# Gate and up of a feed-forward layer: seven block products for eight over half of the contraction

## Chip, cores and metric

One Trainium2 chip, one of its cores. The metric is the time of one execution on the device in microseconds (us). Engines: TensorE (PE; PEld is its weight load), VectorE (DVE), ScalarE (ACT), GpSimd (POOL) and SyncE (SP), which issues the loads of the weights.

## What is computed

One layer of a hybrid encoder for 256 tokens of width 2048, all in float32: a joint input projection, three mixers (a gated recurrence, a stick-breaking attention, a latent attention), an output projection with a residual, and the feed-forward layer that the change is about, whose inner width is 5632:

```python
x = x + jnp.concatenate([hg_out, sb_out, mla_out], axis=-1) @ w_o[layer]
h = rmsnorm(x, ffn_norm_g[layer])
x = x + (jax.nn.silu(h @ w_gate[layer]) * (h @ w_up[layer])) @ w_down[layer]
return rmsnorm(x, final_norm_g)
```

## The kernel before

**Products.** A float32 product is made of three products of a shorter format (float32r). Every operand is split into a rounded part `hi` and a rest `lo`, and `gemm_mm` (L143) sums hi x hi, hi x lo and lo x hi in PSUM (L151 to L153). The weights come in slabs of 256 rows by 512 columns, in SBUF a tile `raw` of 128 partitions x 2 x 512. `split_w` (L105) loads a slab on SyncE's queue (L116), ScalarE casts it to `hi` (L119) and VectorE subtracts to get `lo` (L91, the helper `tt`). There are four buffers each of `raw`, `hi` and `lo`. One slab is 12 products of 128x512: two blocks of 128 rows of tokens (`b`), two halves of the 256 rows (`j`), three products.

**Gate and up.** The inner width is walked in 11 groups of 512 columns. For each group `ff` runs eight slabs of w_gate into two accumulators, then eight slabs of w_up into two others (psA, four banks). ScalarE applies SILU to the gate sums (L835), with the row's norm factor `r2` as scale, VectorE multiplies with the up sums to `hh` (L94), and `turn_hid` transposes `hh` in eight 128x128 blocks (L246) and splits the result into `hi` and `lo` right away: a cast (L827) and a subtraction. A group is 16 slabs, so 192 products, and eight transposes.

**Around it.** The output projection ends in `wo_end`, which adds the residual into the tiles `x2` (R0 to R3), takes sums of squares and makes the transposed copy `x2T`, a tile of hi and lo for each 256 rows. Down (four column blocks of 22 slabs) reads the split hidden tiles and adds into x2; the final norm follows.

**What sets the order.** The program is written as one stream. The framework's scheduler puts each instruction on its engine's list and adds the waits; a buffer of a pool is taken in turn, and its next user waits until the last one is done. `split_w` works under a raised priority (L107, `ahead`), so that loads and splits stand earlier in the lists than the text has them. Small pieces of work (transposes) are kept as tasks that `tick` advances after every slab. An engine runs its list strictly in order. GpSimd has nothing to do in gate and up.

Of the kernel before, what the change touches and what calls it, by code (L numbers as in the profile page):

```python
# [52 lines left out]
SABBUFS = 3  # L53
WARM = 9
MAGIC = 12582912.0
LOGEXP = "natural_log_exp_and_others"


def build(tc, x, xT, pos, gains, fgain, lbraw, w_in, w_uq, w_ukv, w_o, w_gate, w_up, w_down, cst, msk, out, dbg=None):
# [41 lines left out]

# [75 lines left out]

# [1 line left out]
    gcol = cons.tile([P, G_END], F32, name="gcol")  # L179
# [10 lines left out]

# [1 line left out]
    zeros = big("sab", (P, 512), BF16, bufs=SABBUFS)  # L192
# [617 lines left out]

    # ==== gated feed-forward ====
    hid = {}

    def ff(w, c0):
        a = acc_tile()
        for i in range(8):
            gemm_slab(a, w, i * 256, c0, 512, x2T[i], i == 0, i == 7)
        return a

    def turn_hid(g, hh):  # L820
        yield
        for i in range(2):
            ps = transpose4([[hh[:, b, (2 * i + j) * P:(2 * i + j + 1) * P] for b in range(2)] for j in range(2)])
            n = 2 * g + i
            at = act_tile() if n < 8 else late.tile([P, 2, 2, 256], F32R, name=nm("ht"), tag="ht", bufs=14)
            pv = ps.rearrange("p (j n) -> p j n", j=2)
            act.copy(at[:, 0, :, :], pv)  # L827
            tt(at[:, 1, :, :], pv, at[:, 0, :, :].bitcast(F32), ALU.subtract)
            hid[n] = at

    for g in range(11):
        a = ff(w_gate, g * 512)
        sg = late.tile([P, 2, 512], F32, name=nm("sg"), tag="sg", bufs=1)
        for b in range(2):
            act.activation(sg[:, b, :], a[b], AF.Silu, scale=r2[:, b:b + 1])  # L835
        a = ff(w_up, g * 512)
        hh = late.tile([P, 2, 512], F32, name=nm("hh"), tag="hh", bufs=1)
        for b in range(2):
            stt(hh[:, b, :], a[b], r2[:, b:b + 1], sg[:, b, :], ALU.mult, ALU.mult)
        spawn(turn_hid(g, hh))  # L840

    gf = late.tile([P, D], F32, name="gf", bufs=1)
    sp.dma_start(gf, fgain.partition_broadcast(P))
    ss3 = sm(10, "ss3", 1)

    def settle(g, b, a, cs, col):
        tb = x2[g][:, b, cs]
        tt(tb, tb, a[b][:, cs], ALU.add)
        junk = late.tile([P, 512], F32, name=nm("junk"), tag="junk", bufs=1)
        act.activation(junk[:, cs], tb, AF.Square, accum_out=ss3[:, 5 * b + col:5 * b + col + 1])  # L850

    def finish_rows(b, cols):
        ssum = sm(1)
        dve.tensor_reduce(ssum, ss3[:, 5 * b:5 * b + cols], axis=AX.X, op=ALU.add)
# [12 lines left out]
    for g in range(4):
        a = acc_tile()
        held = 4 if g == 3 else 0
        for k in range(22 - held):  # L870
            gemm_slab(a, w_down, k * 256, g * 512, 512, hid[k], k == 0, k == 21)
        if not held:
            for b in range(2):
                settle(g, b, a, whole, g)
                tb = x2[g][:, b, :]
                tt(tb, tb, gf[:, g * 512:(g + 1) * 512], ALU.mult)
            continue
# [78 lines left out]
```

## Time and profile before

| what | value |
|---|---|
| median of 3 runs | 1159.03 us (1157.92 to 1159.41) |
| span of the profiled execution | 1157.1 us |
| TensorE busy | 1133.9 us (98%) |
| VectorE busy | 629.7 us (54%) |
| ScalarE busy | 547.1 us (47%) |
| GpSimd busy | 111.0 us (10%) |
| read from HBM | 208.04 MB, 182 GB/s over the span |

The profile is one execution as the hardware recorded it. Busy time is the time in which an engine had an instruction under way; products overlap, so a busy TensorE may still be spaced by something else, and its pace is read from the starts of its products. The column "idle before" of a row is the engine's idle time just ahead of the instruction, with what ended it.

### The profile page before, as it was taken

To read this page: it belongs to the slowest core of one execution; us is meant where nothing else is said; L and a number is where in the kernel's file an instruction comes from. 1 tells how busy PE (TensorE), PEld (TensorE's weight loads), DVE (VectorE), ACT (ScalarE), POOL (GpSimd) and SP (SyncE) were. 2 spreads that over 40 slices of the span, in tenths; PEclk is the share of its full clock that TensorE was granted. 3 is DMA by queue.
4 is the path that set the end of the run, shared out by engine and by line. 5 is a ranking of instruction groups with operands and counts; after the bars stand their busy time and mean duration, and the time that the engine had idled before them with its cause. 6 is when DMAs were issued, how large, how long until landed. Compare 5 with 4: busy or idle time off the path is not lost.

```text
span 1157.1 us, 14140 instructions
## 1 busy us (share of the span) xinstructions
PE 1133.9 (98%) x5421; PEld 954.9 (83%) x5421; DVE 629.7 (54%) x703; ACT 547.1 (47%) x710; POOL 111.0 (10%) x110
## 2 busy tenths in 40 slices
PE   8989999999999999999999999999999999999997
PEld 4877799999988888888888888888888888888885
DVE  7799655455555554454454554554554545454543
ACT  7654465566645544434444444444444334343432
POOL 3499600011100000000000000000000000000000
PEclk9999999999999999999999999999999999999999
DMA  7633465634665566666666656565566666666662
GB/s 251 228 128 126 144 180 177 179 110 149 197 224 184 182 187 194 187 193 188 191 187 194 188 184 197 183 198 185 185 196 185 191 187 189 193 185 196 185 193 97
DMA packets 71956, 211.07 MB, mean 182 GB/s; under 512 B 7120, under 2 KB 24400, under 8 KB 71760
## 3 DMA queue, kind: packets, MB, share of 16 engines
q1 hardware_dynamic: 71888, 210.17, 58.9%
q8 instruction: 42, 0.69, 0.2%
q14 instruction: 26, 0.21, 0.1%
HBM read 208.04 MB, written 2.10 MB: 182 GB/s over the span
## 4 chain that ended last, share of the span: by engine, by line
PE 88%; POOL 7%; issue 2%; ACT 1%; DVE 1%; DMA 1%; SPq 0%; POOLq 0%; ACTq 0%; DVEq 0%
PE acc L151 27%; PE acc L152 27%; PE acc L153 27%; POOL sA L164 2%; POOL sA L166 2%; POOL cs L160 2%; PE bank L246 2%; POOL sA L160 1%; PE bank L696 1%; DMA L<-xT 1%; PE acc L574 0%; PE acc L573 0%; PE acc L572 0%; PE bank L695 0%; ACT hi L119 0%
## 5 line engine op out<-in xcount | busy, mean ns | idle before, releaser
L91 DVE TENSOR_TENSOR lo<-raw,hi 128x1024 fp32r<-128x1024 f32 (+3 forms) x410 | 484.7, 1185 | 475.9 <-ACT hi L119 475.6
L119 ACT CAST hi<-raw 128x1024 fp32r<-128x1024 f32 (+3 forms) x410 | 409.0, 1000 | 518.9 <-PE acc L153 512.0
L151 PE MATMUL acc<-hi,at 128*128 128x512 f32 (+2 forms) x1352 | 516.8, 383 | 1.2 <-ACT hi L119 1.2
L152 PE MATMUL acc<-lo,at 128*128 128x512 f32 (+2 forms) x1352 | 513.9, 380 | 2.9 <-DVE lo L91 2.8
L153 PE MATMUL acc<-hi,at 128*128 128x512 f32 (+2 forms) x1352 | 512.8, 380 | 0.0
L152 PEld LDWEIGHTS acc<-lo,at 128*128 128x128 f32 x1352 | 254.0, 188 | 50.0 <-DVE lo L91 7.4
L151 PEld LDWEIGHTS acc<-hi,at 128*128 128x128 f32 x1352 | 253.8, 188 | 46.7 <-ACT hi L119 2.9
L153 PEld LDWEIGHTS acc<-hi,at 128*128 128x128 f32 x1352 | 253.8, 188 | 43.5
L175 POOL TENSOR_TENSOR sm<-sm,expo 128x4 f32<-128x4 f32 (+2 forms) x14 | 12.0, 859 | 895.2 <-DVE sm L100 895.2
L152 PE MATMUL acc<-lo,ht 128*128 128x512 f32 (+1 forms) x232 | 89.8, 387 | 0.0
L151 PE MATMUL acc<-hi,ht 128*128 128x512 f32 (+1 forms) x232 | 89.8, 387 | 0.0
L153 PE MATMUL acc<-hi,ht 128*128 128x512 f32 (+1 forms) x232 | 89.8, 387 | 0.0
L152 PEld LDWEIGHTS acc<-lo,ht 128*128 128x128 f32 x232 | 43.5, 187 | 10.0
L151 PEld LDWEIGHTS acc<-hi,ht 128*128 128x128 f32 x232 | 43.5, 187 | 9.9
L153 PEld LDWEIGHTS acc<-hi,ht 128*128 128x128 f32 x232 | 43.5, 187 | 9.9
L156 ACT ACTIVATE at<-bank,gcol 128x256 fp32r<-128x256 f32 x38 | 16.7, 470 | 14.2 <-DVE at L94 13.1
L160 POOL TENSOR_TENSOR cs<-cs,sA 128x256 f32<-128x256 f32 x19 | 21.9, 1152 | 1.2
L94 DVE SCALAR_TENSOR_TENSOR at<-bank,gcol,at 128x256 fp32r<-128x256 f32 x38 | 17.2, 479 | 3.5 <-ACT at L156 3.5
L835 ACT ACTIVATE sg<-acc,sm 128x512 f32<-128x512 f32 x22 | 15.1, 684 | 3.0 <-PE acc L153 3.0
L94 DVE SCALAR_TENSOR_TENSOR hh<-acc,sm,sg 128x512 f32<-128x512 f32 x22 | 15.4, 744 | 0.0
L166 POOL TENSOR_SCALAR sA<-cs 128x256 f32<-128x256 f32 x10 | 14.7, 1473 | 0.9
L388 ACT ACTIVATE R<-R 128x1024 f32<-128x1024 f32 x6 | 6.4, 1064 | 17.2 <-DVE R L91 17.2
(194 smaller groups left out, 543.1 us busy)
## 6 DMA issues: line engine op xcount, KB each, us to landing
raw<-w_gate SPq DMA_DIRECT2D x88, 512.0 KB, 3.5
raw<-w_up SPq DMA_DIRECT2D x88, 512.0 KB, 3.5
raw<-w_down SPq DMA_DIRECT2D x88, 512.0 KB, 4.3
raw<-w_in SPq DMA_DIRECT2D x48, 384.0 KB, 3.9
raw<-w_in SPq DMA_DIRECT2D x32, 512.0 KB, 3.6
raw<-w_o SPq DMA_DIRECT2D x32, 512.0 KB, 3.6
raw<-w_in SPq DMA_DIRECT2D x16, 256.0 KB, 5.2
raw<-w_in SPq DMA_DIRECT2D x8, 320.0 KB, 3.4
```

The costliest lines, as they stand in the source:

```text
L91: dve.tensor_tensor(o, a, b, op=op)
L94: dve.scalar_tensor_tensor(o, a, s, b, op0=op0, op1=op1)
L119: act.copy(hi[:, js, :n], raw[:, js, :n])
L151: pe.matmul(o, lhsT=ah, rhs=hi[:, j, cs], start=start and j == 0, stop=False)
L152: pe.matmul(o, lhsT=ah, rhs=lo[:, j, cs], start=False, stop=False)
L153: pe.matmul(o, lhsT=al, rhs=hi[:, j, cs], start=False, stop=stop and j == 1)
L156: act.activation(dst[:, 0, j, :], src, AF.Copy, scale=g)
L160: pool.tensor_tensor(o, a, b, op=op)
L164: pool.tensor_scalar(o, a, s1, None, op0=op0)
L166: pool.tensor_scalar(o, a, s1, s2, op0=op0, op1=op1)
L246: pe.transpose(ps[:, j * 256 + b * P: j * 256 + (b + 1) * P], s, K[:, K_ID:K_ID + P])
L835: act.activation(sg[:, b, :], a[b], AF.Silu, scale=r2[:, b:b + 1])
```

## The change

Half of the contraction of gate and up, the first four of eight slabs (`FAST = 4`), is computed as a 2x2 block product in Winograd's form of Strassen's method. The two rows of blocks are the two halves of the tokens, the inner pair is the two halves of a slab's 256 rows, and the two columns are the gate slab and the up slab of the same place. Seven products of 128x128 by 128x512 take the place of eight, each still three products of float32r: 21 instead of 24. For that

- four sums of weight blocks, T0 to T3, are made for each of these pairs of slabs (`fast_weights`): T0, T1 and T3 on GpSimd (`ptt`), T2 on VectorE (`tt`), and split into `hT` and `lT` like weights;
- the matching sums of activation blocks are made once, in `wo_end`;
- four of the seven products go to four banks of psM (p1, p6, p7, p5), three straight to the accumulators c11, c21, c12; the four banks are combined by ScalarE and VectorE after the fourth unit;
- gate and up of the other four slabs are computed as before, but side by side (`plain_unit`), into c11, c21, c12, c22;
- the products of gate and up are kept as fp32 (`hidf`) in free tiles, among them R0 to R3, and split into hi and lo only in the first column block of down (`split_hid`); x2 is saved to DRAM in `wo_end` on ScalarE's queue and loaded again there.

```diff
-    actp = es.enter_context(tc.tile_pool(name="actp", bufs=16))
+    actp = es.enter_context(tc.tile_pool(name="actp", bufs=18))
...
+        kept = dram.tile([P, 2, 512], F32, name=nm("kept"), tag=f"kept{g}", bufs=1)
+        act.dma_start(kept, t)
...
+                A = ffp.tile([P, 8, P], F32, name=nm("T"), tag="T")
                 for j in range(2):
-                    split_act(at, j, ps[:, j * 256:(j + 1) * 256], gc(G_FFN, 4 * g + 2 * i + j))
-                x2T[2 * g + i] = at
+                    act.activation(A[:, 2 * j:2 * j + 2, :], ps[:, j * 256:(j + 1) * 256].rearrange("p (b n) -> p b n", b=2),
+                                   AF.Copy, scale=gc(G_FFN, 2 * n + j))
+                tt(A[:, 4, :], A[:, 1, :], A[:, 3, :], ALU.add)
+                tt(A[:, 5, :], A[:, 4, :], A[:, 0, :], ALU.subtract)
+                tt(A[:, 6, :], A[:, 1, :], A[:, 0, :], ALU.subtract)
+                tt(A[:, 7, :], A[:, 2, :], A[:, 5, :], ALU.subtract)
...
+                act.copy(ah, A)
+                tt(al, A, ah.bitcast(F32), ALU.subtract)
+                x2T[n] = (ah, al)
...
+    def load(w, r0, c0, spare=False):
+        if spare:
+            raw = ffp.tile([P, 2, 512], F32, name=nm("rawb"), tag="rawb", bufs=RAWS)
+        else:
+            raw = slabp.tile([P, 2, 512], F32, name=nm("raw"), tag="raw", bufs=RAWS)
...
+    def halve(src, js, hi=None, lo=None):
...
+        act.copy(hi[:, js, :], src[:, js, :])
+        tt(lo[:, js, :], src[:, js, :], hi[:, js, :].bitcast(F32), ALU.subtract)
...
+    def fast_weights(wa, wb, r0, c0):
+
+        with tc.high_priority(offset=ahead[0]):
+            ra, rb = load(wa, r0, c0), load(wb, r0, c0, True)
+            T = ffp.tile([P, 4, 512], F32, name=nm("T"), tag="T")
+            ptt(T[:, 0, :], rb[:, 0, :], ra[:, 0, :], ALU.subtract)
+            ptt(T[:, 1, :], rb[:, 0, :], rb[:, 1, :], ALU.subtract)
+            tt(T[:, 2, :], rb[:, 1, :], T[:, 0, :], ALU.subtract)
+            ptt(T[:, 3, :], ra[:, 1, :], T[:, 2, :], ALU.subtract)
+            a = halve(ra, slice(0, 2))
+            b = halve(rb, slice(1, 2))
...
+    PRODUCTS = (("p1", 0, 0, 0), ("p6", 5, 2, 2), ("p7", 6, 2, 1), ("p5", 4, 2, 0),
+                ("c11", 2, 0, 1), ("c21", 3, 2, 3), ("c12", 7, 1, 1))
...
+        act.copy(u1, accs["p1"])
+        tt(u2, u1, accs["p6"], ALU.add)
+        tt(u3, u2, accs["p7"], ALU.add)
+        tt(u2, u2, accs["p5"], ALU.add)
+        tt(u4, u3, accs["p5"], ALU.add)
+        for i in range(FAST, 8):
+            with tc.high_priority(offset=ahead[0]):
+                wa = halve(load(w_gate, i * 256, g * 512), slice(0, 2))
+                wb = halve(load(w_up, i * 256, g * 512, True), slice(0, 2))
+            plain_unit(accs, wa, wb, x2T[i], i == FAST, i == 7)
...
+        for b, (ug, cg, uu, cu) in enumerate(((u1, "c11", u2, "c12"), (u3, "c21", u4, "c22"))):
+            tt(ug, ug, accs[cg], ALU.add)
+            act.activation(ug, ug, AF.Silu, scale=r2[:, b:b + 1])
+            tt(uu, uu, accs[cu], ALU.add)
+            stt(uu, uu, r2[:, b:b + 1], ug, ALU.mult, ALU.mult)
...
+            if g == 0:
+                with tc.high_priority(offset=ahead[0]):
+                    split_hid(k)
```

**VectorE at the end of a group.** Before, the splits of the slabs (`lo`) follow each other, with the two multiplications `hh` between them:

```order
L91 TENSOR_TENSOR lo_6980<-raw_6978,hi_6979 128x1024
L91 TENSOR_TENSOR lo_6998<-raw_6996,hi_6997 128x1024
L91 TENSOR_TENSOR lo_7032<-raw_7030,hi_7031 128x1024
L94 SCALAR_TENSOR_TENSOR hh_6973<-acc_6827,sm_3830,sg_6824 128x512
L94 SCALAR_TENSOR_TENSOR hh_6973<-acc_6828,sm_3830,sg_6824 128x512
L91 TENSOR_TENSOR lo_7050<-raw_7048,hi_7049 128x1024
```

Now VectorE has at the same place (`rawb` are up slabs, `T` the sums of weights; `s`, `u` and `v` hold the group's sums and `acc` is a PSUM accumulator of the plain units):

```order
L93 TENSOR_TENSOR lo_4554<-rawb_4551,hi_4553 128x1024
L93 TENSOR_TENSOR lo_4599<-raw_4589,hi_4598 128x1024
L93 TENSOR_TENSOR T_4733<-rawb_4731,T_4733 128x512
L93 TENSOR_TENSOR lo_4603<-rawb_4591,hi_4602 128x512
L93 TENSOR_TENSOR s_900_4415<-s_900_4415,acc_4258 128x512
L93 TENSOR_TENSOR u_901_4416<-u_901_4416,acc_4259 128x512
L93 TENSOR_TENSOR lo_4651<-raw_4641,hi_4650 128x1024
L93 TENSOR_TENSOR u_902_4417<-u_902_4417,acc_4260 128x512
L93 TENSOR_TENSOR v_4418<-v_4418,acc_4261 128x512
L93 TENSOR_TENSOR lo_4655<-rawb_4643,hi_4654 128x512
L96 SCALAR_TENSOR_TENSOR u_902_4417<-u_902_4417,sm_3864,s_900_4415 128x512
L96 SCALAR_TENSOR_TENSOR v_4418<-v_4418,sm_3864,u_901_4416 128x512
```

The first row is the up half of the group's last plain unit, the third is T2 of the next group's fourth fast unit, and the four additions that read `acc` stand behind it, with the gate slab of the next group's second unit between the second and the third.

**GpSimd in gate and up.** Before, GpSimd's list has the norm factor ahead of gate and up and the next row only in the final norm:

```order
L175 TENSOR_TENSOR sm_3830<-sm_3828,expo 128x2
L175 TENSOR_TENSOR sm_8908<-sm_8906,expo 128x1
```

Now T0, T1 and T3 of every fast unit stand between the two, 12 rows a group:

```order
L177 TENSOR_TENSOR sm_3864<-sm_3862,expo 128x2
L162 TENSOR_TENSOR T_4235<-rawb_4233,raw_4231 128x512
L162 TENSOR_TENSOR T_4235<-rawb_4233 128x512
```

Both inputs of the last row are halves of one up slab. Nothing of GpSimd's was moved; these rows were added.

## Rows read from the trace of the kernel before

**Rows 1.** The page, part 1: busy us, share of the span, instructions.

```profile
PE 1133.9 (98%) x5421; PEld 954.9 (83%) x5421; DVE 629.7 (54%) x703; ACT 547.1 (47%) x710; POOL 111.0 (10%) x110
```

**Rows 2.** One group: stretch, length, busy us (instructions), clock, DMA share, GB/s.

```profile
481.50:526.00 44.50, 44.50 (x202) 36.94 (x201) 22.20 (x21) 19.15 (x20) 0.00 (x0) 1.00 0.62 189
```

**Rows 3.** Timeline of TensorE in gate and up: start us, us, instruction.

```profile
458.36 0.39 PE L153 MATMUL acc<-hi,at 128*128 128x512 f32 x1
...
461.08 0.39 PE L153 MATMUL acc<-hi,at 128*128 128x512 f32 x1
```

**Rows 4.** The chain that ended last: start us, us, what; two groups' transposes.

```profile
464.87 0.87 PE bank L246 x8
...
909.14 0.87 PE bank L246 x8
```

**Rows 5.** Timeline of VectorE where GpSimd is at rest, back to back.

```profile
138.25 2.35 DVE L91 TENSOR_TENSOR lo<-raw,hi 128x1024 fp32r<-128x1024 f32 x2
140.52 0.48 DVE L94 SCALAR_TENSOR_TENSOR at<-bank,gcol,at 128x256 fp32r<-128x256 f32 x1
...
28.06 1.28 DVE L91 TENSOR_TENSOR lo<-raw,hi 128x512 fp32r<-128x512 f32 x2
29.27 0.48 DVE L94 SCALAR_TENSOR_TENSOR at<-L,gcol,at 128x256 fp32r<-128x256 f32 x1
```

**Rows 6.** Timelines of VectorE and GpSimd in the first stage, at the same times.

```profile
17.68 2.37 DVE L91 TENSOR_TENSOR lo<-raw,hi 128x512 fp32r<-128x512 f32 x2
...
20.77 3.49 DVE L91 TENSOR_TENSOR lo<-raw,hi 128x512 fp32r<-128x512 f32 x2
...
18.15 1.36 POOL L228 TENSOR_TENSOR scx<-scx,on 128x512 f32<-128x512 f32 x1 [1.07 <-ACT on L227]
...
20.52 1.49 POOL L228 TENSOR_TENSOR scx<-scx,on 128x512 f32<-128x512 f32 x1 [1.01 <-ACT on L227]
...
22.37 1.34 POOL L228 TENSOR_TENSOR scx<-scx,on 128x512 f32<-128x512 f32 x1 [0.36 <-ACT on L227]
```

**Rows 7.** 60 to 120 us: groups by form (busy us, mean ns), two stretches, timelines.

```profile
L91 DVE TENSOR_TENSOR lo<-raw,hi 128x1024 fp32r<-128x1024 f32 x16 | 22.9, 1436 | 0.0
...
L160 POOL TENSOR_TENSOR cs<-cs,sA 128x256 f32<-128x256 f32 x14 | 16.1, 1147 | 0.8
...
L160 POOL TENSOR_TENSOR sA<-sA,sA 128x256 f32<-128x256 f32 x7 | 7.5, 1065 | 0.6
...
60.00:90.00 30.00, 26.31 (x136) 22.82 (x136) 29.11 (x34) 17.31 (x25) 28.17 (x25) 0.94 0.38 123
90.00:120.00 30.00, 27.32 (x140) 22.24 (x139) 30.00 (x38) 12.63 (x14) 28.17 (x26) 1.00 0.44 141
...
91.53 0.79 POOL L160 TENSOR_TENSOR cs<-cs,sA 128x256 f32<-128x256 f32 x1
...
91.66 0.73 DVE L406 COPY_PREDICATED qk<-msk,bank 128x512 f32<-128x512 int32 x1
92.28 1.21 DVE L91 TENSOR_TENSOR R<-R,L 128x512 f32<-128x512 f32 x2
```

**Rows 8.** Groups by form from 500 to 900 us: busy us, mean ns, idle before.

```profile
L91 DVE TENSOR_TENSOR lo<-raw,hi 128x1024 fp32r<-128x1024 f32 x145 | 177.7, 1225 | 202.2 <-ACT hi L119 202.2
L119 ACT CAST hi<-raw 128x1024 fp32r<-128x1024 f32 x144 | 152.1, 1057 | 224.7 <-PE acc L153 224.7
...
L835 ACT ACTIVATE sg<-acc,sm 128x512 f32<-128x512 f32 x18 | 12.3, 684 | 2.7 <-PE acc L153 2.7
```

**Rows 9.** The page, part 6: DMA issues, count, KB each, median us to landing.

```profile
raw<-w_up SPq DMA_DIRECT2D x88, 512.0 KB, 3.5
```

**Rows 10.** TensorE's longest wait, and the two stretches of 3 us behind it.

```profile
63.32 1.64 PE L354 MATMUL bank<-cst,R 128*128 128x128 f32 x8 [4.39 <-DVE R L91]
...
63.00:66.00 3.00, 2.68 (x14) 2.68 (x15) 2.97 (x4) 1.39 (x4) 2.83 (x3) 0.64 0.48 167
66.00:69.00 3.00, 3.00 (x18) 2.78 (x17) 2.15 (x4) 1.95 (x5) 2.75 (x4) 0.79 0.47 171
```

More of the change, by code (lines that the diff above doesn't have):

```diff
@@ L54 @@
 WARM = 9
+RAWS = 4
+FAST = 4
 MAGIC = 12582912.0
@@ L774, in build @@
     mix.__exit__(None, None, None)
-    late = es.enter_context(tc.tile_pool(name="late", bufs=2))
+    dram = es.enter_context(tc.tile_pool(name="dram", bufs=1, space=bass.MemoryType.DRAM))
+    x2kept = []
+    ffp = es.enter_context(tc.tile_pool(name="ffp", bufs=2))
     def wo_end(a, g):
@@ L809, in build @@
     r2 = rsqrt_mean(ssum, D, 2)
-    hid = {}
[L814 to L842, printed above, removed]
@@ new lines, in build, with fast_unit @@
+    PRODUCTS = (("p1", 0, 0, 0), ("p6", 5, 2, 2), ("p7", 6, 2, 1), ("p5", 4, 2, 0),
+                ("c11", 2, 0, 1), ("c21", 3, 2, 3), ("c12", 7, 1, 1))
+    def fast_unit(accs, ws, forms, start):
+        ah, al = forms
+        for name, f, which, k in PRODUCTS:
+            hi, lo = ws[which]
+            o = accs[name]
+            last = name[0] == "p" and start == "last"
+            pe.matmul(o, lhsT=ah[:, f, :], rhs=hi[:, k, :], start=start is True, stop=False)
+            pe.matmul(o, lhsT=ah[:, f, :], rhs=lo[:, k, :], start=False, stop=False)
+            pe.matmul(o, lhsT=al[:, f, :], rhs=hi[:, k, :], start=False, stop=last)
@@ new lines, in plain_unit @@
+    def plain_unit(accs, wa, wb, at, start, stop):
+        for nme, b, (hi, lo) in (("c11", 0, wa), ("c21", 1, wa), ("c12", 0, wb), ("c22", 1, wb)):
+            o = accs[nme]
+            for j in range(2):
+                ah = at[:, 0, j, b * P:(b + 1) * P]
+                al = at[:, 1, j, b * P:(b + 1) * P]
+                pe.matmul(o, lhsT=ah, rhs=hi[:, j, :], start=start and nme == "c22" and j == 0, stop=False)
+                pe.matmul(o, lhsT=ah, rhs=lo[:, j, :], start=False, stop=False)
+                pe.matmul(o, lhsT=al, rhs=hi[:, j, :], start=False, stop=stop and j == 1)
@@ new lines, in part, with turn_hid @@
+    def part(tag, bufs=1):
+        return ffp.tile([P, 512], F32, name=nm(tag), tag=tag, bufs=bufs)
+    def turn_hid(g, hs):
+        if g < 6:
+            f = actp.tile([P, 2, 512], F32, name=nm("at"), tag="at")
+        elif g < 10:
+            f = rt(g - 6)
+        else:
+            f = ffp.tile([P, 2, 512], F32, name=nm("hf"), tag="hf", bufs=1)
+        for i in range(2):
+            ps = transpose4([[hs[b][:, (2 * i + j) * P:(2 * i + j + 1) * P] for b in range(2)] for j in range(2)])
+            act.copy(f[:, i, :], ps)
+            hidf[2 * g + i] = f[:, i, :]
+            yield
@@ new lines, in build @@
+    hidf = {}
+    for g in range(11):
+        accs = {}
+        for i in range(FAST):
+            ws = fast_weights(w_gate, w_up, i * 256, g * 512)
+            if not accs:
+                for n in ("p1", "p6", "p7", "p5"):
+                    accs[n] = bank()
+                for n in ("c11", "c21", "c12", "c22"):
+                    accs[n] = acc1()
+            fast_unit(accs, ws, x2T[i], True if i == 0 else "last" if i == FAST - 1 else False)
+        u1, u3, u2, u4 = part("s1"), part("u3"), part("u2", 2), part("v", 2)
+        act.copy(u1, accs["p1"])
[8 more added lines that the diff above has]
+            plain_unit(accs, wa, wb, x2T[i], i == FAST, i == 7)
+            if g == 0 and i == FAST:
+                flush()
+            tick()
+        for b, (ug, cg, uu, cu) in enumerate(((u1, "c11", u2, "c12"), (u3, "c21", u4, "c22"))):
[3 more added lines that the diff above has]
+            stt(uu, uu, r2[:, b:b + 1], ug, ALU.mult, ALU.mult)
+        spawn(turn_hid(g, (u2, u4)))
@@ L844, in build, with split_hid @@
+    hid = {}
+    pairs = []
+    def split_hid(n):
+        if n < 18:
+            at = act_tile()
+        else:
+            if n % 2 == 0:
+                pairs.append(ffp.tile([P, 2, 2, 2, 256], F32R, name=nm("T"), tag="T"))
+            at = pairs[-1][:, n % 2]
+        f = hidf[n].rearrange("p (j n) -> p j n", j=2)
+        act.copy(at[:, 0, :, :], f)
+        tt(at[:, 1, :, :], f, at[:, 0, :, :].bitcast(F32), ALU.subtract)
+        hid[n] = at
     ss3 = sm(10, "ss3", 1)
@@ L870, in build @@
         for k in range(22 - held):
-            gemm_slab(a, w_down, k * 256, g * 512, 512, hid[k], k == 0, k == 21)
+            if g == 0:
+                with tc.high_priority(offset=ahead[0]):
+                    split_hid(k)
+                if k in (14, 16, 18, 20):
+                    i = (k - 14) // 2
+                    x2[i] = rt(i)
+                    sp.dma_start(x2[i], x2kept[i])
+            gemm_slab(a, w_down, k * 256, g * 512, 512, hid[k], k == 0, k == 21)
+        if g == 0:
+            for i in range(2):
+                t = ffp.tile([P, 2, 512], F32, name=nm("hT"), tag="hT")
+                sp.dma_start(t, fgain[i * 1024:(i + 1) * 1024].partition_broadcast(P))
+                gf += [t[:, 0, :], t[:, 1, :]]
         if not held:
@@ L875, in build @@
                 tb = x2[g][:, b, :]
[L876 removed]
+                tt(tb, tb, gf[g], ALU.mult)
             continue
```

36 lines of the change are left out of this document (29 added, 7 removed).

## The prediction

> **What bounds the kernel now.** I read the busy times first, then the stretches of gate and up, then single instructions. TensorE is busy 98% of the span, VectorE 54%, GpSimd 10% [rows 1]; over a whole column group of gate and up TensorE has no idle time, VectorE works 22.2 of 44.5 us and GpSimd does nothing, at the full granted clock [rows 2]. The reader should see there that TensorE sets the end of this stage and that every product left out is worth its spacing. That spacing: the third product of a quarter starts at 458.36 and the one twelve products later at 461.08, so 0.2267 us each [rows 3]. A group is 192 products and eight transposes, 43.5 + 0.9 = 44.4; in the chain of waits the transposes come back every (909.14 - 464.87) / 10 = 44.43 us [rows 4]. Eleven groups are 489 us of the 1157.1.
>
> **What it removes.** A group becomes 4 x 21 + 4 x 24 = 180 products. The built programs hold 132 products of 512 columns fewer (4008 to 3876). 132 x 0.2267 = 29.9 us if TensorE stays the bound: a group of 40.8 + 0.9 = 41.7 us.
>
> **What it adds to VectorE.** I call a group's Strassen units u1 to u4, its plain ones p5 to p8, the four sums of weights T0 to T3. Splits of 128x1024: eight for p5 to p8, four for the gate slabs of u1 to u4, eight for the T's: 20. Of 128x512: four splits of the up halves, four T2, eight additions from PSUM, two multiplications: 18. Back to back a 1024-wide split takes (140.52 - 138.25) / 2 = 1.135 us, a 512-wide one (29.27 - 28.06) / 2 = 0.605 [rows 5]. So 22.7 + 10.9 = 33.6 us a group where there were 22.2. Alone that fits under 41.7.
>
> **GpSimd's share.** It gets 12 TENSOR_TENSOR of 128x512 a group, both inputs in SBUF, while VectorE works. Gate and up of before show nothing like it, but the first stage shows the same shape on both engines: GpSimd's takes 1.34 to 1.49 us, and two 512-wide splits of VectorE that take 1.28 us in a pair elsewhere take 2.37 where they meet one of GpSimd's, 3.49 where they meet two [rows 5, 6]. Each such GpSimd instruction costs VectorE 1.09 to 1.11 us; I use 1.09. Half-width ones agree: from 60 to 120 us, with GpSimd never at rest, sixteen splits of 1024 took 1.436 us each where 1.225 is usual [rows 7, 8], 16 x 0.21 = 3.4 us more; they are 16 x 1.135 = 18.2 of VectorE's 59.1 busy us there, and 21 GpSimd TENSOR_TENSOR at half of 1.09, times 18.2 / 59.1, make 3.5. The cost falls only where VectorE has both inputs in SBUF: a COPY_PREDICATED of 512 with one input in PSUM, begun under a GpSimd TENSOR_TENSOR, let the next instruction start 92.28 - 91.66 = 0.62 us later [rows 7], as if alone. Ends for the price: 0 (all 12 fall on VectorE's PSUM additions and waits) and 1.09 each; I take 1.09 for 11 of 12, since 28.8 of the 33.6 us have two SBUF inputs and one of the 12 is waited for by VectorE itself: 12.0 us.
>
> [...]
>
> **Waits that the order forces on VectorE.** Two, seen in the order. (1) It splits u2's gate slab between the second and third addition of the former group's plain sums. ScalarE casts that slab only after a SILU that needs the first addition: 0.68 + 1.06 [rows 8] less the second addition's 0.6 leaves 1.1 us idle. (2) T2 of the next u4 stands in VectorE's queue ahead of u1's last split and of all those additions. It waits for GpSimd's T0, that for the up slab, and that slab is loaded into the buffer which VectorE frees with p8's last split: 3.5 us to land [rows 9] and 1.34 for T0, less one other split of 1.135, leaves 3.7 us. Who waits behind it: u1's seventh product needs the accumulator that the third addition frees, so TensorE stops there. A group for VectorE: 33.6 + 12.0 + 1.1 + 3.7 = 50.4 us. This closes on itself: p8's split, T2 of u4, the four units' splits, p5's split, u1's load and T's, p7's split, u3's load, p8's split. TensorE, at 41.7, waits out the rest.
>
> **The sum.** From one group's first product to the next's 50.4 instead of 44.43: ten such, +59.7. The last group makes no T for another: 41.7 and the stop at u1's seventh product. There p8's last split is followed by 3.5 + 1.34 + 0.6 to the end of T2 and by u1's last split, three additions, wait 1 and u2's split, 4.7: 10.1 us, plus two GpSimd instructions that meet them, 2.2, while TensorE has 12 + 18 products, 6.8: a stop of 5.5, so 47.2, +2.8. The first group's T's are made during the output projection, with its up slabs loaded earlier than later groups': wait 2 smaller, an estimated -2. Together +60.5. The profiled execution has a span of 1157.1, and the median of the timed runs, 1159.03, is 1.9 above that: 1159 + 60 = 1219.
>
> **Edits costed at nothing.** ScalarE gets some 27 us a group (20 casts of 1.06 and small ones) under either pace. The split of the hidden values moves into the first column of down: 0.605 + 1.135 us of VectorE a slab against 12 x 0.2267 = 2.72 of TensorE; uncovered it would cost 22 x 0.6 = 13. Saving and reloading the residual is eight transfers of 512 KB more, on queues with a DMA share of 0.62 [rows 2]. The up slabs loaded ahead wait in SyncE's queue for the same last transposes as the load of the final gain did, with w_o loads behind; those have four buffers of cover. The wider transposed copies add some 2 us of VectorE to each of four slabs of the output projection, where it has 1.5 us of slack a slab; bound 0 to 4, taken at 0.
>
> **Rivals.** (A) No contention to speak of: GpSimd's work falls into VectorE's gaps. VectorE then needs 33.6 + 4.8 = 38.4 us a group, TensorE sets the pace at 41.7 with small stops, and the change brings nearly all of 29.9: 1131. For it: 13 us of VectorE's time need not meet GpSimd. Against: all seven GpSimd instructions of that shape in the first stage met two-input work of VectorE, and all cost it time; three of them stand in [rows 6]. It decides at (44.4 - 38.4) / 12 = 0.5 us per GpSimd instruction: below that the kernel is faster than before, above slower. (B) Half of them meet: 33.6 + 6 + 4.8 = 44.4 a group, no change but the ends: 1160. [...] (D) That the products aren't left out: the count of the programs excludes it.
>
> **How the numbers follow.** The forecast, 0.62, with its own range 1185 to 1248 (price 0.8 to 1.3). A 0.16, B and what lies between B and the forecast 0.14, C 0.08. The range from 1155 to 1250 leaves out A and the upper end of C. Faster by over 0.2% (about what a measurement of this kernel can tell from no change, 2.3 us): A and the lower edge of B, 0.18; within: 0.04; slower: 0.78.
>
> **What would show it.** Right: groups of 48 to 53 us; VectorE's 1024-wide splits at 1.3 us or more on average; idle time of VectorE ended by GpSimd's T; TensorE waiting for VectorE at the up accumulator of the first unit, in pieces of about 5.5 us, with a lower clock behind. Wrong: splits at 1.23 and groups of 41.7, or TensorE waiting elsewhere, for loads above all. The price per GpSimd instruction is the number on which it all hangs: it was measured on pairs of 512-wide instructions, not on a queue in which GpSimd may lose its turn instead.

## The result and the profile after

The changed kernel takes 1228.45 us (median of four runs, 1227.09 to 1230.67) where the kernel before takes 1159.22: a ratio of 1.0602, 95% interval 1.0587 to 1.0617, 6% slower. The forecast was 1219 with 1155 to 1250 around it. The profiled execution has a span of 1226.7 us, 69.6 more than before. One run of all those below, the fourth of the kernel with two units and its sums on VectorE, took 2662.7 us and is left out.

The page of the changed kernel, part 1 (busy us, share of the span, instructions), to set beside [rows 1]:

```profile
PE 1144.0 (93%) x5289; PEld 944.5 (77%) x5289; DVE 885.9 (72%) x935; ACT 623.5 (51%) x835; POOL 338.0 (28%) x242
```

TensorE has 132 products fewer, as the diff says, and is busy for 10 us more, because part of them ran at a lower clock (the mean granted clock is 0.968, where it was 0.997). GpSimd's 132 new instructions add 227 us of busy time, 1.7 us each.

**Where the 69.6 us lie.** The starts of TensorE's products, counted off in groups, give the stages. Timeline of TensorE in the changed kernel: the first product of gate and up, of the second group, of the last group, and of down:

```profile
414.81 0.39 PE L882 MATMUL bank<-hi,at 128*128 128x512 f32 x1
...
471.53 0.39 PE L882 MATMUL bank<-hi,at 128*128 128x512 f32 x1
...
927.44 0.39 PE L882 MATMUL bank<-hi,at 128*128 128x512 f32 x1
...
976.28 0.39 PE L153 MATMUL acc<-hi,at 128*128 128x512 f32 x1
```

The same in the kernel before, first product of gate and up and of down:

```profile
414.85 0.39 PE L151 MATMUL acc<-hi,at 128*128 128x512 f32 x1
...
903.53 0.39 PE L151 MATMUL acc<-hi,at 128*128 128x512 f32 x1
```

Gate and up went from 488.7 to 561.5 us (+72.8), down and the end from 253.6 to 250.4 (-3.2). The first group takes 56.7 us, the nine in the middle (927.44 - 471.53) / 9 = 50.66, the last 48.8; before, each took 44.4.

**One middle group.** VectorE, while the next group's sums are made, T2 of its u1 first and T2 of its u4 last (start us, us, instruction, idle time before and its releaser), beside [rows 5, 8]:

```profile
650.95 1.76 DVE L93 TENSOR_TENSOR T<-rawb,T 128x512 f32<-128x512 f32 x1 [1.64 <-POOL T L162]
...
655.09 2.32 DVE L93 TENSOR_TENSOR lo<-raw,hi 128x1024 fp32r<-128x1024 f32 x1
657.33 2.31 DVE L93 TENSOR_TENSOR lT<-T,hT 128x1024 fp32r<-128x1024 f32 x1
659.56 1.21 DVE L93 TENSOR_TENSOR lo<-rawb,hi 128x1024 fp32r<-128x1024 f32 x1
...
675.02 1.76 DVE L93 TENSOR_TENSOR T<-rawb,T 128x512 f32<-128x512 f32 x1 [2.98 <-POOL T L162]
...
677.90 0.68 DVE L93 TENSOR_TENSOR u<-u,acc 128x512 f32<-128x512 f32 x1
679.70 1.22 DVE L93 TENSOR_TENSOR lo<-raw,hi 128x1024 fp32r<-128x1024 f32 x1 [1.13 <-ACT hi L851]
```

GpSimd in the same group:

```profile
649.63 1.29 POOL L162 TENSOR_TENSOR T<-rawb,raw 128x512 f32<-128x512 f32 x1 [23.09 <-DMA rawb<-w_up]
650.88 1.29 POOL L162 TENSOR_TENSOR T<-rawb 128x512 f32<-128x512 f32 x1
...
654.04 2.29 POOL L162 TENSOR_TENSOR T<-rawb,raw 128x512 f32<-128x512 f32 x1
656.28 2.27 POOL L162 TENSOR_TENSOR T<-rawb 128x512 f32<-128x512 f32 x1
...
676.86 1.66 POOL L162 TENSOR_TENSOR T<-raw,T 128x512 f32<-128x512 f32 x1 [0.63 <-DVE T L93]
```

A split of 1024 that takes 1.21 us alone takes 2.31 beside a GpSimd instruction: 1.09 more. GpSimd's own instruction takes 1.29 alone and 2.27 beside a split. From 654 to 660 us the two lists are in step, and each waits for one instruction of the other. The addition from PSUM at 677.90 runs under GpSimd's third sum and keeps its 0.68. In this group nine VectorE instructions are longer, by 0.67 to 1.10 us and 9.3 in all.

VectorE idles there for T2 twice (1.64 for u1's, 2.98 for u4's) and 1.13 behind the SILU. Over a longer stretch of middle groups (stretch, length, then busy us of PE, PEld, DVE, ACT, POOL, clock, DMA share, GB/s), beside [rows 2]:

```profile
480.00:890.00 410.00, 365.14 (x1501) 287.02 (x1500) 350.01 (x305) 198.08 (x232) 164.91 (x96) 0.94 0.52 165
```

410 us are 8.09 groups of 50.66: VectorE is busy 43.2 us in each and idle 7.4.

It is a loop, and stands in the chain that ended last (start us, us, what):

```profile
643.03 1.23 DVE lo L93
644.28 5.18 DMA rawb<-w_up
649.63 2.54 POOL T L162 x2
...
666.89 1.77 DVE T L93
668.67 1.15 DVE lo L93
669.83 3.70 DMA rawb<-w_up
673.70 1.30 POOL T L162
...
681.67 0.47 PE acc L882
...
692.34 1.06 ACT hi L851
...
693.43 1.24 DVE lo L93
```

The up split of p5, the load of u1's up slab into its buffer, its sums, splits; the up split of p8, u4's load, its sum, and round again to p5's split: it is the loop that the prediction closed, but with a stretch that the prediction left out. From u1's seventh product (681.67) to 692.3 the chain runs over 46 of TensorE's products, one after the other: ScalarE's cast of p5's up slab, the row at 692.34, waits until TensorE has read a buffer of `hi`. VectorE has its list full in that stretch too and waits 0.16 us for the cast. TensorE's waits in this group:

```profile
664.80 0.50 PE L893 MATMUL acc<-lo,at 128*128 128x512 f32 x1 [0.55 <-DVE lo L93]
...
669.86 0.50 PE L893 MATMUL acc<-lo,at 128*128 128x512 f32 x1 [2.03 <-DVE lo L93]
...
678.03 0.50 PE L882 MATMUL acc<-hi,at 128*128 128x512 f32 x1 [1.00 <-DVE s L93]
...
681.67 0.47 PE L882 MATMUL acc<-hi,at 128*128 128x512 f32 x1 [1.98 <-DVE u L93]
```

And its clock (the number ahead of the DMA share) in the two stretches of 3 us behind the wait of 2.03, beside [rows 10]:

```profile
670.00:673.00 3.00, 3.00 (x9) 2.39 (x10) 2.04 (x1) 0.00 (x0) 0.96 (x1) 0.62 0.44 169
673.00:676.00 3.00, 3.00 (x12) 2.36 (x12) 0.98 (x1) 0.00 (x0) 2.31 (x2) 0.81 0.54 180
```

The products there are 0.43 us apart for a while, where [rows 3] have 0.2267. In this group that only takes the place of waiting, because the chain is not on TensorE at that time. In six of the eight such loops between 520 and 900 us it is: the lower clock reaches into the 46 products of the chain. One of these six, then the group shown (columns as above):

```profile
578.23:590.65 12.42, 12.42 (x46) 10.02 (x47) 10.80 (x13) 7.12 (x10) 0.00 (x0) 0.85 0.72 225
681.67:692.35 10.68, 10.68 (x46) 8.64 (x47) 10.68 (x13) 7.12 (x10) 0.00 (x0) 1.00 0.76 236
```

The same products take 1.7 us more at a clock of 0.85, and VectorE stands idle 1.8 us behind three casts (0.86 + 0.77 + 0.16) where it stood 0.16. So TensorE's stops cost VectorE time in most groups, by way of the clock and the buffers of `hi`.

### The profile page after: what moved, and what is told of

Same layout as the page of the kernel before. It is cut to its first block, busy times and chain, and to the rows that moved or that the text cites. A ratio compares the mean times of both kernels' runs of the same rounds, so it can differ in the third digit from the quotient of the medians.

```text
span 1226.7 us, 14499 instructions
## 1 busy us (share of the span) xinstructions
PE 1144.0 (93%) x5289; PEld 944.5 (77%) x5289; DVE 885.9 (72%) x935; ACT 623.5 (51%) x835; POOL 338.0 (28%) x242
## 4 chain that ended last, share of the span: by engine, by line
PE 53%; POOL 13%; issue 12%; DVE 10%; DMA 7%; ACT 4%; SPq 0%; POOLq 0%; ACTq 0%; DVEq 0%
PE acc L153 12%; PE acc L154 12%; PE acc L155 12%; DMA rawb<-w_up 6%; POOL T L162 6%; DVE lo L93 4%; DVE lT L93 2%; DVE T L93 2%; POOL sA L166 2%; PE bank L882 2%; PE bank L883 2%; PE bank L884 2%; PE acc L882 2%; ACT hT L851 2%; POOL cs L162 2%
## 5 line engine op out<-in xcount | busy, mean ns | idle before, releaser
L121 ACT CAST hi<-raw 128x1024 fp32r<-128x1024 f32 (+3 forms) x234 | 222.7, 956 | 236.0 <-PE acc L155 222.1
L154 PE MATMUL acc<-lo,at 128*128 128x512 f32 (+2 forms) x808 | 302.3, 374 | 3.0 <-DVE lo L93 2.9
L153 PE MATMUL acc<-hi,at 128*128 128x512 f32 (+2 forms) x808 | 304.0, 378 | 1.1 <-ACT hi L121 0.9
L155 PE MATMUL acc<-hi,at 128*128 128x512 f32 (+2 forms) x808 | 301.3, 373 | 0.0
L153 PEld LDWEIGHTS acc<-hi,at 128*128 128x128 f32 x808 | 151.6, 188 | 25.3 <-ACT hi L121 2.3
L155 PEld LDWEIGHTS acc<-hi,at 128*128 128x128 f32 x808 | 151.7, 188 | 22.0
L893 PE MATMUL acc<-lo,at 128*128 128x512 f32 x352 | 142.4, 405 | 19.5 <-DVE lo L93 18.8
L894 PE MATMUL acc<-hi,at 128*128 128x512 f32 x352 | 141.2, 401 | 4.1 <-DVE at L96 4.1
L93 DVE TENSOR_TENSOR lT<-T,hT 128x1024 fp32r<-128x1024 f32 x88 | 138.6, 1576 | 6.0 <-ACT hT L851 5.7
L892 PE MATMUL acc<-hi,at 128*128 128x512 f32 x352 | 142.0, 403 | 0.0
L851 ACT CAST hT<-T 128x1024 fp32r<-128x1024 f32 x88 | 92.3, 1049 | 96.7 <-POOL T L162 96.7
L851 ACT CAST hi<-raw 128x1024 fp32r<-128x1024 f32 x88 | 92.0, 1046 | 61.6 <-PE acc L884 58.5
L162 POOL TENSOR_TENSOR T<-raw,T 128x512 f32<-128x512 f32 x44 | 80.7, 1835 | 47.3 <-DVE T L93 47.3
L93 DVE TENSOR_TENSOR lo<-rawb,hi 128x512 fp32r<-128x512 f32 (+1 forms) x88 | 84.6, 962 | 1.9 <-ACT hi L851 1.8
L894 PEld LDWEIGHTS acc<-hi,at 128*128 128x128 f32 x352 | 68.1, 193 | 19.7 <-DVE at L96 5.6
```

Source lines behind the costliest of these rows:

```text
L93: dve.tensor_tensor(o, a, b, op=op)
L153: pe.matmul(o, lhsT=ah, rhs=hi[:, j, cs], start=start and j == 0, stop=False)
L154: pe.matmul(o, lhsT=ah, rhs=lo[:, j, cs], start=False, stop=False)
L155: pe.matmul(o, lhsT=al, rhs=hi[:, j, cs], start=False, stop=stop and j == 1)
L162: pool.tensor_tensor(o, a, b, op=op)
L851: act.copy(hi[:, js, :], src[:, js, :])
```

## The experiments

The theory, L: a GpSimd instruction that reads SBUF stops VectorE's two-input work for about as long as it runs, and that lifts VectorE above TensorE. The rivals: W, the waits that the order makes (VectorE behind GpSimd's T0 and the loads) are the cause; V, VectorE's own added work is enough. In the recorded expectations t_dve is the first kernel below, fast2 the one with two units and its sums on GpSimd, and cand1 the one with the first group's copies first and the sums on VectorE.

**The sums on VectorE.**

```diff
-            ptt(T[:, 0, :], rb[:, 0, :], ra[:, 0, :], ALU.subtract)
-            ptt(T[:, 1, :], rb[:, 0, :], rb[:, 1, :], ALU.subtract)
+            tt(T[:, 0, :], rb[:, 0, :], ra[:, 0, :], ALU.subtract)
+            tt(T[:, 1, :], rb[:, 0, :], rb[:, 1, :], ALU.subtract)
...
-            ptt(T[:, 3, :], ra[:, 1, :], T[:, 2, :], ALU.subtract)
+            tt(T[:, 3, :], ra[:, 1, :], T[:, 2, :], ALU.subtract)
```

> The three sums of weights T0, T1 and T3 go from GpSimd to VectorE; nothing else is changed. Theory L (a GpSimd instruction of that shape stops two-input work of VectorE): VectorE gets 12 x 0.605 = 7.3 us a group more and loses 9.3 us of stretching and the part of its waits that was GpSimd's own work (2.6 of some 6.5 us), so the middle groups fall from 50.7 us to about 45.5, the first by about 8, and the time to 1155 to 1175 us. Rival W (it is the order's waits alone, and GpSimd loses its turn instead of VectorE): only the 2.6 us go, the 7.3 come on top, groups of 55 us, about 1280. Rival V (VectorE's own added work is what binds): slower than 1228 as well.

Measured: 1144.0 us, ratio 0.9876 (0.9861 to 0.9891). Twelve more instructions a group on the engine that was the bound, and the kernel is 84 us faster than the changed one and 14 faster than the one before. V falls. W is not settled by this run, because the waits go with the sums (VectorE's idle time falls from 7.4 to 0.8 us a group); the copies below settle it. The middle groups take 42.23 us. The same stretch as above:

```profile
480.00:890.00 410.00, 410.00 (x1828) 334.77 (x1827) 402.32 (x488) 252.32 (x297) 0.00 (x0) 1.00 0.65 201
```

VectorE is full (402 of 410 us), TensorE too. It went below the range that L gave, because L left some 4 us of waiting in each group (6.5 - 2.6) and there is under 1: with T0 to T3 in one list, no sum waits for GpSimd, and the up slabs have landed when VectorE gets to them. One loss is left, in the first group (55.0 us): a single wait of TensorE, in its timeline

```profile
458.51 0.79 PE L894 MATMUL acc<-hi,at 128*128 128x512 f32 x1 [10.79 <-DVE at L96]
```

for the last transposed copies of x2, which stand in VectorE's list behind the raised splits and sums of the second group.

**GpSimd busy, but not reading.**

```diff
-            ptt(T[:, 0, :], rb[:, 0, :], ra[:, 0, :], ALU.subtract)
-            ptt(T[:, 1, :], rb[:, 0, :], rb[:, 1, :], ALU.subtract)
+            pool.memset(T[:, 0, :], 0.0)
+            pool.memset(T[:, 1, :], 0.0)
...
-            ptt(T[:, 3, :], ra[:, 1, :], T[:, 2, :], ALU.subtract)
+            pool.memset(T[:, 3, :], 0.0)
```

> GpSimd writes zeros into T0, T1 and T3 instead of the sums of weights, so that the values of these three sums are left out; it has as many instructions as before, but none reads SBUF, and none waits for a load. All splits and products stay. Theory L: no stretching of VectorE, only T2's wait for its own load and the 1.1 us wait are left: VectorE 33.6 + 1.1 + 2 to 4, so TensorE sets the pace at 41.7 plus stops of 1 to 2 us, and the time is 1130 to 1145 us, with VectorE's 1024-wide splits at 1.23 us in the row of the trace. Rival V (VectorE's own work binds): stays above 1200. If GpSimd's writing alone takes VectorE's turn, the splits stay at 1.5 us and the groups at 46 us or more.

Measured: 1130.5 us, ratio 0.9758 (0.9743 to 0.9772); every group 42.1 us, the first and the last too, and no wait of TensorE in gate and up. Groups of VectorE by form from 470 to 880 us (busy us, mean ns, idle before):

```profile
L93 DVE TENSOR_TENSOR lo<-raw,hi 128x1024 fp32r<-128x1024 f32 x80 | 97.9, 1224 | 45.8 <-ACT hi L851 44.6 <-ACT hi L121 1.1
L93 DVE TENSOR_TENSOR lT<-T,hT 128x1024 fp32r<-128x1024 f32 x73 | 89.0, 1220 | 5.2 <-ACT hT L851 5.2
```

1.22 us each, beside 105 writes of GpSimd of 0.53 us in that stretch, where [rows 8] have 1.225: GpSimd's writing costs VectorE nothing here. VectorE hardly waits for GpSimd here either (0.9 us of the same 410 as above), so this kernel shows what the change would bring without the blocking and without those waits: 28 us.

**The same waits, shorter reading.**

```diff
-            ptt(T[:, 0, :], rb[:, 0, :], ra[:, 0, :], ALU.subtract)
-            ptt(T[:, 1, :], rb[:, 0, :], rb[:, 1, :], ALU.subtract)
+            pool.tensor_copy(T[:, 0, :], rb[:, 0, :])
+            pool.tensor_copy(T[:, 1, :], rb[:, 1, :])
...
-            ptt(T[:, 3, :], ra[:, 1, :], T[:, 2, :], ALU.subtract)
+            pool.tensor_copy(T[:, 3, :], T[:, 2, :])
```

> GpSimd copies one block into T0, T1 and T3 each instead of subtracting two, so that the second terms of these sums are left out; the instructions wait for the same loads and for T2 as before, and read SBUF through one input. A one-input instruction of GpSimd of this shape took 0.62 us in the kernel before. Theory L with a lock for any reading of SBUF: each stops VectorE for about its own time, so the stretching halves to about 4 to 5 us a group and groups are 43 to 46 us: 1145 to 1180. If only two-input work of GpSimd stops VectorE: no stretching, 33.6 + 1.1 + 4 to 5 of waits, TensorE's 41.7 with stops: 1130 to 1145. Rival W (the waits for GpSimd and the loads, not the stretching): 50.7 less some 2 x 0.7 a group, above 1210.

Measured: 1150.0 us, ratio 0.9924 (0.9908 to 0.9941), groups of 43.2 us. VectorE still waits for GpSimd nearly as long as in the changed kernel: 3.5 us a group between 480 and 890 us, where it was 4.2 (0.88, 0.51 and 2.79 us in one group). What is gone is the length of the blocking. GpSimd, then VectorE, in that group:

```profile
661.55 0.61 POOL L861 COPY T<-rawb 128x512 f32<-128x512 f32 x1
...
666.06 1.60 POOL L861 COPY T<-rawb 128x512 f32<-128x512 f32 x1
```

```profile
664.42 1.22 DVE L93 TENSOR_TENSOR lo<-raw,hi 128x1024 fp32r<-128x1024 f32 x1
665.56 1.63 DVE L93 TENSOR_TENSOR lT<-T,hT 128x1024 fp32r<-128x1024 f32 x1
```

A copy of 0.61 us costs a split 0.41, where a subtraction of 1.29 cost 1.09: 0.2 less than the instruction's length in both. So one-input reading blocks as well, and the price goes with the length of GpSimd's instruction. VectorE has 33.6 us of work, 0.6 of hidden tiles' splits, 3.2 of blocking (what is left of its busy time; the seven longer instructions of the group shown make 2.8) and 5.8 of idle time, 43.2, just above TensorE's own 42.1. W falls as the sole cause: it had above 1210. The waits alone would not have cost the change its gain.

**T2 on GpSimd too**, so that VectorE waits for no sum in person:

```diff
-            tt(T[:, 2, :], rb[:, 1, :], T[:, 0, :], ALU.subtract)
+            ptt(T[:, 2, :], rb[:, 1, :], T[:, 0, :], ALU.subtract)
```

> T2 goes to GpSimd too, so that VectorE no longer waits for GpSimd with a sum of weights, and GpSimd has 16 instead of 12 instructions a group. Theory L (GpSimd's reading stops VectorE): VectorE 33.6 - 2.4 = 31.2, stretching 16 x 0.78 (9.3 us over 12 instructions in the changed kernel) = 12.4, the 1.1 us wait, and 2 to 4 us in which splits wait for the sums: 47 to 49 us a group, 1190 to 1215 us, the 1024-wide splits at 1.5 us or more. Rival W (the waits behind GpSimd's T0 and the loads are the cause): these go, groups of 42 to 43 us and 1130 to 1150 us.

Measured: 1212.7 us, ratio 1.0468 (1.0454 to 1.0482), middle groups 49.7 us: the time lies where L had it, the groups 0.7 us above its range, and W's range is far off. The wait has only moved to the splits of the sums, now behind ScalarE's cast of them (VectorE is idle 7.5 us a group, where it was 7.4), and the blocking takes in more. One of VectorE's multiplications, which took 0.75:

```profile
672.54 1.78 DVE L96 SCALAR_TENSOR_TENSOR u<-u,sm,s 128x512 f32<-128x512 f32 x1
```

**A fifth buffer for the up slabs.**

```diff
-            raw = ffp.tile([P, 2, 512], F32, name=nm("rawb"), tag="rawb", bufs=RAWS)
+            raw = ffp.tile([P, 2, 512], F32, name=nm("rawb"), tag="rawb", bufs=RAWS + 1)
...
-            f = ffp.tile([P, 2, 512], F32, name=nm("hf"), tag="hf", bufs=1)
+            f = ffp.tile([P, 2, 512], F32, name=nm("hf"), tag="hT")
```

> The up slabs get a fifth buffer (its place comes from the last group's hidden tile, which now shares one with the split sums); GpSimd's and VectorE's work is unchanged. Theory L: the load of an up slab no longer waits for the split of the slab four before it, only for SyncE's turn behind the gate slab's load, one split earlier, 1.2 to 2.3 us at each of two places in a group; groups go from 50.7 to 46 to 48.5 us and the time to 1180 to 1210 us, since the 9.3 us of stretching stay. Rival W: most of the 6.5 us of waits go and with them the loss: below 1170. If SyncE's order holds the load all the same: 1228, no change.

Measured: 1198.3 us, ratio 1.0346 (1.0332 to 1.0360), middle groups 47.3 us. The stretch again:

```profile
480.00:890.00 410.00, 380.86 (x1635) 301.98 (x1634) 370.30 (x327) 214.87 (x250) 199.27 (x103) 0.98 0.57 177
```

8.67 groups: busy 42.7 us in each, idle 4.6 where it was 7.4. So the waits are worth 2.8 to 3.4 us a group on top of the blocking, which stays; both theories' parts are real, and they add up on VectorE. The first group got longer, 60.5 us where it was 56.7.

**Two of eight units instead of four, sums on GpSimd, then on VectorE.**

```diff
-FAST = 4
+FAST = 2
```

> Two of eight units with seven products instead of four, so 186 products a group, six GpSimd instructions, all as in the changed kernel otherwise. Theory L: VectorE 18 x 1.135 + 14 x 0.605 = 28.9, stretching 6 x 0.78 = 4.7, waits up to 6.5: 40 us, under TensorE's 186 x 0.2267 + 0.9 = 43.1: TensorE sets the pace again with small stops, groups of 43.1 to 44, and the time is 1135 to 1152 us. Rival W (each group pays the waits at its border whatever VectorE's load is): 43.1 + 4 or more, above 1180.

Measured: 1163.9 us, ratio 1.0046 (1.0032 to 1.0060): neither range holds it. The groups take 45.2 us, though VectorE is idle over 9 us in each. Averages hide the place: between 661 and 681 us of one group VectorE waits for two sums

```profile
665.39 1.77 DVE L93 TENSOR_TENSOR T<-rawb,T 128x512 f32<-128x512 f32 x1 [2.56 <-POOL T L162]
...
674.41 1.77 DVE L93 TENSOR_TENSOR T<-rawb,T 128x512 f32<-128x512 f32 x1 [1.18 <-POOL T L162]
```

and loses some 4.6 us to GpSimd's six instructions there, so that the splits of two plain units come late and TensorE stops 0.39 and 0.95 us for them. The same kernel with T0, T1 and T3 on VectorE, as in the first experiment:

> fast2 with T0, T1 and T3 on VectorE. fast2 took 45.2 us a group, 2.1 over TensorE's own 43.1, although VectorE was idle 9.5 us a group: one stop of TensorE of 1.3 us behind a stretch of some 18 us in which VectorE waited for GpSimd's sums (2.6 and 1.2 us) and lost 5 us to GpSimd's instructions. Theory L: without GpSimd neither is there, VectorE has 28.9 + 6 x 0.605 = 32.5 us, groups of 43.1 to 43.4 us and 1139 to 1146 us. Rival: the stop comes from the place of the splits in VectorE's list, not from GpSimd: groups stay at 45 us or rise, 1160 or more.

Measured: 1143.3 us, ratio 0.9873 (0.9853 to 0.9893), every middle group 43.28 us, no wait of TensorE. The late splits were GpSimd's doing, not the list's.

**The other half of the change alone**: gate and up as before, the hidden product kept as fp32. No unit is in Winograd's form (`FAST = 0`), so the wider transposed copies are left out too; the later loads of the final gain, which the list of the change leaves unnamed, are in.

```diff
+    for g in range(11):
+        a = ff(w_gate, g * 512)
...
+        a = ff(w_up, g * 512)
+        hh = [part("u2", 2), part("v", 2)]
+        for b in range(2):
+            stt(hh[b], a[b], r2[:, b:b + 1], sg[b], ALU.mult, ALU.mult)
+        spawn(turn_hid(g, hh))
```

> Only the second part of the change: gate and up as in the kernel before (192 products a group, gate slabs, then up slabs, no sums of weights), the hidden product kept as fp32 and split in the first column of down, the residual saved and loaded again. Theory: this part costs nothing, since the stage of down was 3 us shorter after the change than before: 1152 to 1163 us. Rival: the 22 splits in the first column of down and the eight transfers are part of the 69 us, with up to 13 to 24 us: 1172 or more.

Measured: 1155.2 us, ratio 0.9973 (0.9962 to 0.9983): it costs nothing and brings 3 us, all of them in down (903.39 to the end at 1153.5, 250.1 where 253.6 stood).

**The first group's copies first.** The sums on VectorE, and

```diff
             if g == 0 and i == FAST:
-                flush()
+                with tc.high_priority(offset=ahead[0]):
+                    flush()
```

> T0, T1 and T3 on VectorE as in t_dve, and the last transposed copies of x2, which the first group's plain units need, get the raised priority that the splits have. In t_dve TensorE stood still 10.8 us for them in the first group, whose other work took 44.2; with that gone and the other groups at 42.2: 1131 to 1136 us. If VectorE, which has hardly a gap there, only pays the copies later: 1140 to 1145, no change against t_dve.

Measured: 1134.7 us, ratio 0.9796 (0.9783 to 0.9810): 2% under the kernel before and 94 us under the changed one, and no version that computes everything was measurably faster. The first group takes 42.4 us. The same edit without moving the sums:

> The changed kernel with the raised priority for the last transposed copies alone; the sums of weights stay on GpSimd. The first group took 56.7 us where the middle ones took 50.7; TensorE stood 4.1 us for these copies in it. If the copies' place is what made the first group long, it falls to about 50 and the time to 1220 to 1224 us. If the loss is VectorE's stretching by GpSimd at the end of the output projection (2.2 + 2.4 us of stops there, before the copies) and VectorE has no slack, the copies only change places with splits: 1226 to 1230.

Measured: 1228.7 us, ratio 1.0606 (1.0588 to 1.0623): nothing. The first two groups together take 101.8 us, where they took 103.1. With VectorE as the bound here, a better order in its list only changed which of its customers waits. And the kernel of 1134.7 us with the first group's four additions raised as well:

```diff
+        with tc.high_priority(offset=ahead[0] if g == 0 else 0):
-        tt(u2, u1, accs["p6"], ALU.add)
...
+            tt(u2, u1, accs["p6"], ALU.add)
```

> cand1, and the first group's four additions of products from the four banks get the raised priority too: in cand1 TensorE waited 2.2 us for the last of them at the start of the second group, which took 44.6 us instead of 42.2. That gone: 1131 to 1133 us. If it only comes back elsewhere: 1134 to 1136, no change against cand1.

Measured: 1134.3 us, ratio 0.9791 (0.9776 to 0.9806): no change. The wait of 2.2 us that it was meant for is gone from the second group, and four others, 3.3 us together, stand in its place there and in later groups; the second group takes 43.5 us where it took 44.6, the third 43.2 where it took 42.1.

## Why the prediction was right, and what in it was not

**The signs.** Groups of 50.7 us, 1024-wide splits of 1.52 us on average (161 of them between 480 and 890 us, 244.2 us), idle time ended by GpSimd's T, and a lower clock behind TensorE's stops (0.62 and 0.81 behind the one of 2.03) are there as forecast. Stops of 5.5 us in one piece are not.

**What was removed** was sized well: 41.7 us a group from TensorE's spacing; the kernel with GpSimd's writes alone ran at 42.1, and the rest is in the last section.

**VectorE's own work**, 33.6 us: in that same kernel it is busy 339.7 us in 9.74 groups, 34.9, of which 1.3 are splits of the hidden tiles that the stretch takes in. Right.

**GpSimd's price**, 1.09 us: right to the digit when it meets two-input work (2.31 against 1.22). How often it meets was put too high: nine of twelve in the group shown, not eleven, for 9.3 us there and 9.6 a group by difference over the long stretch (43.2 - 33.6), instead of 12.0. The other three ran into waits and PSUM additions. Where the runs put the border: a split of 1024 takes 2.31 us beside a GpSimd sum and 1.22 beside the writes, and the addition from PSUM keeps its 0.68. GpSimd's whole time is not what VectorE loses: 1.09 of the sum's 1.29, 0.41 of the copy's 0.61.

**The forced waits** were put too low: 4.8 us against 7.4. What VectorE waited for between 480 and 890 us, 8.09 groups (us in total, times, longest us):

```profile
DVE T L93 <- POOL T L162: 34.1, 16, 4.0
DVE lo L93 <- ACT hi L851: 19.3, 27, 1.1
```

The wait behind SILU is right (1.1 against 1.13). T2's wait for GpSimd was found once in the loop (3.7); the trace has it twice (1.64 + 2.98 in the group shown, 4.2 a group in the first row), because at two places of the loop, u1 and u4, a load waits for the split of an up slab and T2 for the load, and up slabs land later in company (4.2 us in the median, where [rows 9] have 3.5). That is 0.5 of the 2.6 us missed. The rest are waits that the prediction did not have: 1.3 us a group for casts that wait until TensorE has read a buffer of `hi` (the second row less eight waits of 1.13 behind SILU), and 0.6 for the first cast of the sums. The prediction's loop ran over VectorE alone, with TensorE only waiting it out. The two wrong sizes, -2.4 and +2.6, cancel: 50.66 measured, 50.4 forecast. The sum was right partly by luck.

**TensorE's stops** were worked out for the last group, as one of 5.5 us at the seventh product of u1. There the trace has 3.7 in two pieces (2.39 and 1.35), and 3.0 us more than the products need at full clock. In the middle groups 8.7 us were to be waited out (50.4 - 41.7); the stops are 5.6 in the group shown, in four pieces at three kinds of place, and the slower products again take some 3.0 (50.66 - 42.1 - 5.6).

**The first group** is the step that failed: forecast at 48.4 with a gain of 2, measured 56.7. Its sums were seen only as waiting less for loads. In fact the sums of its four units are made nearly in one run, 401 to 426 us, beside VectorE's last splits of the output projection and its first of gate and up, and most of them meet two-input work. GpSimd, then TensorE there:

```profile
404.51 2.21 POOL L162 TENSOR_TENSOR T<-raw,T 128x512 f32<-128x512 f32 x1 [0.63 <-DVE T L93]
406.67 2.28 POOL L162 TENSOR_TENSOR T<-rawb,raw 128x512 f32<-128x512 f32 x1
```

```profile
417.36 0.50 PE L883 MATMUL bank<-lo,at 128*128 128x512 f32 x1 [2.16 <-DVE lo L93]
...
425.50 0.47 PE L882 MATMUL acc<-hi,at 128*128 128x512 f32 x1 [2.37 <-DVE R L93]
...
455.84 0.80 PE L894 MATMUL acc<-hi,at 128*128 128x512 f32 x1 [2.36 <-DVE at L96]
```

These three stops and two smaller ones make 8.6 us, and products at a lower clock (0.91 over the group) take 6.0 more than the 42.1 that they need. With GpSimd only writing, the first group took 42.2 us. With the sums on VectorE it took 55.0 until the copies were raised, and 42.4 then; with GpSimd blocking, raising them brought nothing. So it is VectorE's load at that border first and the copies' place in its list second; the "1.5 us of slack a slab" that the prediction saw there was too little for the sums as well. That the wider copies alone cost next to nothing was right: in the kernel with GpSimd only writing, which has them, gate and up start at 415.25, 0.4 us later than before. The last group was 1.6 us longer than forecast, the middle nine 2.3 together, and down 3.2 shorter: 8.3 + 1.6 + 2.3 - 3.2 = 9.0 of the 9.1 us by which the forecast was short (69.6 against 60.5).

**The rivals.** A, no contention to speak of, is what the kernel with writes alone shows: 1130.5, where A had 1131. The point from which it decides, 0.5 us an instruction, fits: the copies cost 0.41 where they meet, and the kernel came out 8 us under the one before. C, given 0.08, had VectorE lose GpSimd's whole time, a price that no run shows: to a sum of 1.29 us VectorE lost 1.09. What did come on top of the price: up slabs land 0.7 us later (4.2 for 3.5), and the clock behind TensorE's stops costs about 1.7 us in most groups (12.42 for 10.68 us over the 46 products above).

## What to carry to other kernels

A helper engine is not free because it is idle: before moving two-input work to GpSimd, count what VectorE does in the same stretch with two SBUF inputs, and price each meeting at nearly GpSimd's own time (1.09 of 1.29 us for the sums of this kernel, 0.41 of 0.61 for the copies). Here twelve sums cost VectorE 9.6 us from GpSimd and 7.3 us when it did them itself, and the second also took the waits away, 94 us in all with the first group's order mended. With GpSimd blocking VectorE, a better order in VectorE's list gave nothing back and a fifth buffer 30 us; taking the blocking off gave 84, and only then was the order worth 9. Take blocking or work off a full engine first. And follow the chain through the short pieces: the stretch of 46 products, 0.23 us each, is over a fifth of the loop.

## What the runs showed of the hardware that was not expected

- GpSimd loses as much as VectorE: its 128x512 sums take 1.29 us alone (1.25 apart) and 2.2 to 2.3 in step with splits. The prediction asked whether GpSimd "may lose its turn instead"; both lose.
- The price is GpSimd's time less 0.2 us, for the two-input sum (1.29, 1.09) as for the copy (0.61, 0.41). What the 0.2 is, no run shows.
- Products are not all spaced alike at the full clock. Down before, between two products with a hidden tile `ht`, twelve apart:

```profile
1049.99 0.39 PE L153 MATMUL acc<-hi,ht 128*128 128x512 f32 x1
...
1052.80 0.39 PE L153 MATMUL acc<-hi,ht 128*128 128x512 f32 x1
```

(1052.80 - 1049.99) / 12 = 0.234 us, where products with `at` tiles have 0.2267 [rows 3]. Before, 14 of the 22 hidden tiles are `ht`; after, 18 are `at` and 4 others. Ten tiles of 48 products at 0.0075 make 3.6 us, about the 3.2 that down gained. Products that read `hT` or `lT` in gate and up are 0.233 apart too ((644.30 - 642.43) / 8; 48 a group, 0.3 us: the distance from 41.7 to the 42.1 measured). What in these tiles does it, their place or something else, was not tried.
